# Second layer's output projection: seven block products for the heads' rows, on scaled float16 pairs

## The chip, the cores and the metric

The kernel runs on one core of one Trainium2 chip. Its engines work side by side, each through its own queue in order: TensorE (PE) multiplies, VectorE (DVE), ScalarE (ACT) and GpSimd (POOL) work elementwise, SyncE (SP) issues most of the DMAs. The metric is the device time of one execution in microseconds (us); three timed runs of the kernel before gave a median of 1188.93 us (1188.14 to 1191.31). The profile is of one further execution.

## The reference

Two layers of a decoder with 1024 tokens and width 1024. Layer 1 has as its main part a forgetting attention of 16 heads, and beside it a cross-attention of 4 heads into 256 memory tokens. Both are gated, joined and projected:

```python
def mixer_sublayer(x, mem, w_in, w_mem_kv, w_out, main_fn):
    h = x @ w_in
    ...
    y_main = main_fn(u_main)                       # (1024, 1024)
    y_mem = memory_attention(q_mem, mem, w_mem_kv) # (1024, 512)
    y = jnp.concatenate([y_main * jax.nn.silu(g_main), y_mem * jax.nn.silu(g_mem)], axis=-1)
    return y @ w_out                               # w_out: (1536, 1024)

# each layer
x = layer_norm(ALPHA * x + y, ln_g[layer], ln_b[layer])
```

All is float32. `w_out` has 1024 rows for the heads and 512 rows for the memory's heads.

## The kernel before

A float32 product is made of three products of lower precision: each operand is split into a high part and a rest, and high x high, high x rest and rest x high are summed in one PSUM bank. Two splits are in use. `hi_lo` (L195) makes a float32r high part (ACT), a bfloat16 rest (DVE, L199) and a bfloat16 copy of the whole (ACT or POOL). `scaled_hi_lo` (L170) multiplies by a power of two and makes two float16 tensors: ACT writes the high part (L171), DVE the rest (L172). The projections of layer 1 and the attention use float16 pairs; both output projections use `hi_lo`.

`OutProj` (L560) is the output projection. The contraction over 1536 rows of `w_out` is 12 tiles of 128 rows, in three groups `c`: 0 and 1 are the heads, 2 is the memory. The tokens are eight tiles of 128, taken as four pairs `sp`; the columns are two halves of 512 (`nh`). For one pair, four PSUM banks (two tiles x two halves) each collect 12 x 3 matmuls of 128x128 by 128x512: 144 per pair, 576 in all (L615). The gated results `y` go through DRAM (`y1d`) and come back transposed to the projection as tiles of `T`; `w_out` comes in pieces of 128x512 (`fetch_two`, L569) and is split one piece at a time (`split`, L584). When a pair is done, `norm` (L691) adds ALPHA times the residual, takes the statistics (bn_stats on DVE), and applies scale and shift in two DVE instructions of 128x1024 (L710, L712), then a DMA writes the rows out.

In layer 1 the projection begins inside the attention: `fox` (L1174) runs 16 heads and a last stretch of six steps, in which the first pair's memory products (`early`) are laid between the attention's last products. PE's order is written out by hand there (`manual_schedule`); instructions under `keep_in_program_order` are pinned on their engine; the rest is ordered by the framework's scheduler. After `fox`, `rest` (L643) runs the other products in the order pair 0: c 0, then pair 1: c 2, pair 0: c 1, pair 1: c 0 and 1, then pairs 2 and 3. PSUM banks come from named pools: `pj` (2 banks), `L` (3), `T` (2), `O` (1).

The last head pair's result `o` (a tile of `G`) is made by ACT (L1148) and DVE (L1149) out of bank `O`, gated on POOL (L1158, in `pair_out`), and stored to `y1d`.

Of the kernel before, what the change touches and what calls it, by code (L numbers as in the profile page):

```python
# [9 lines left out]
F32 = mybir.dt.float32  # L10
# [8 lines left out]
P = 128  # L19
# [16 lines left out]
LAG = 6  # L36
# [42 lines left out]
def trunk_kernel(ctx, tc, x, xT, memT, win, wk, wv0, wv, wmk, wmv, wout, poolw, pscale, lng, lnb, bforget, out):  # L79
# [30 lines left out]
    def G(shape=(P, S), dt=F32):  # L110
        return sb(list(shape), "G", 4, dt)
# [157 lines left out]
    def power_of(to, m, least):  # L269

        nc.vector.tensor_scalar(m, m, least, None, ALU.max)
        nc.vector.tensor_scalar(to.bitcast(I32), m.bitcast(I32), 0x7F800000, None, ALU.bitwise_and)

    scales = const.tile([P, 20], F32, name="scales")
    ex, sx, sq, unq, unv0, unv, tmp, tmp2 = (scales[:, k : k + 1] for k in range(8))
    ews, sws, un1s, hun1s = ([scales[:, 8 + 3 * k + g : 9 + 3 * k + g] for g in range(3)] for k in range(4))
# [24 lines left out]
    def scales_of_weights(g):  # L301

        m = highest[:, g : g + 1]
        ew, sw, un1, hun1 = ews[g], sws[g], un1s[g], hun1s[g]
        power_of(ew, m, 2.0 ** -24)
        nc.vector.reciprocal(sw, ew)
        nc.vector.tensor_scalar(sw, sw, 2.0 ** 12, None, ALU.mult)
        nc.vector.tensor_tensor(un1, ex, ew, ALU.mult)
        if g == 1:
            nc.vector.tensor_tensor(unq, un1, un1, ALU.mult)  # L310
            nc.vector.tensor_scalar(unq, unq, 2.0 ** -19, None, ALU.mult)
            nc.vector.reciprocal(sq, unq)
        nc.vector.tensor_scalar(un1, un1, 2.0 ** -25, None, ALU.mult)
        nc.vector.tensor_scalar(hun1, un1, 0.5, None, ALU.mult)
        if g == 2:
            for un, a in ((unv0, un1s[1]), (unv, un1)):
                nc.vector.tensor_tensor(un, a, un1, ALU.mult)
                nc.vector.tensor_scalar(un, un, 2.0, None, ALU.mult)

# [240 lines left out]
    class OutProj:  # L560
# [82 lines left out]
        def rest(self, resid, X, dst):  # L643
# [14 lines left out]
            for sp, c in order:  # L658
# [21 lines left out]
                if X is not None and c == 0 and sp in (1, 2):  # L680
                    keep(sp - 1)
                if c == 1:
                    norm(sp, accs.pop(sp), gb, zs, X, dst)

    def rows_of(resid, sp):
        zs = [G() for _ in range(2)]
        for a, z in enumerate(zs):
            tc.keep_in_program_order(nc.sync.dma_start(z, resid[(2 * sp + a) * P : (2 * sp + a + 1) * P, :]))
        return zs

    def norm(sp, accs, gb, zs, X, dst):  # L691
        for a in range(2):
            s = 2 * sp + a
            rows = slice(s * P, (s + 1) * P)
            z = zs[a]
            stats = tiny(12)
            for nh in range(2):
                zn = z[:, nh * NH : (nh + 1) * NH]
                nc.vector.scalar_tensor_tensor(zn, zn, ALPHA, accs[a][nh], ALU.mult, ALU.add)  # L699
                nc.vector.bn_stats(stats[:, 6 * nh : 6 * nh + 6], zn)  # L700
# [7 lines left out]
            nc.vector.tensor_tensor(r, r, t, ALU.mult)  # L708
            for cols in (slice(0, NH), slice(NH, D)) if s == ST - 1 else (slice(0, D),):
# [126 lines left out]
    with tc.tile_pool(name="in1", bufs=1) as in1:  # L836
# [317 lines left out]
        def pair_out(pr, c, o, g):  # L1154

            for k in (2 * c + 1, 2 * c) if g is not None else ():
# [17 lines left out]
        def fox(following, out_proj, head):  # L1174
# [8 lines left out]
            for hd in range(HEADS + 1):  # L1183
# [16 lines left out]
                for i in range(ST if hd < HEADS else LAG):  # L1200
# [40 lines left out]
                    else:  # L1241
                        inverse()
                        behind()
                        out_proj.split(11 + i, True, gp_copy)
                        if i > 1:
                            out_proj.fetch_two(two_lines(4 + 2 * i))
                    if pr == 7:
                        out_proj.split((0, 0, 0, 0, 1, 3, 4, 6, 6, 6, 6, 6, 7, 8, 9, 10)[step], True, gp_copy)
# [5 lines left out]
                    if hd == HEADS and i == LAG - 1:  # L1254
                        out_proj.begin()
# [10 lines left out]
        wtags = [("B", 10), ("V", 4), ("MK", 4)] + [("B", 10)] * 3 + [("w", 0), ("MK", 4), ("R", 2), ("V", 4), ("PG", 0), ("B", 10)]  # L1266
        out_proj = OutProj(1, w_slots(wtags, in1), y1d)
# [10 lines left out]
        out_proj.rest(x1, None, out)  # L1278
# [61 lines left out]
```

## Time and profile before

| | |
|---|---|
| median of three timed runs | 1188.93 us |
| profiled execution, first to last instruction | 1185.0 us |
| what lies around the span in a timed run (1188.93 - 1185.0) | 3.9 us |
| PE, ACT, DVE, POOL busy | 1162.7, 685.3, 780.6, 288.0 us |
| layer 0's output projection on PE | about 340 to 462 us |
| the attention's last product | about 1057 us |
| the last output product | about 1175 us |

The device time of the profiled execution itself is not listed apart from its span. A busy PE need not be a PE at its peak, so spacing of matmuls is read from the starts of consecutive rows. The chain of work that ended last follows PE through the whole of the last 120 us: 48 of its 75 longest pieces after 1044 us are runs of L615, and only the last layer norm stands behind it.

### The profile page before, as it was taken

The numbers are of one execution on the slowest core, as the hardware profiler recorded it, in microseconds if no ns is written. First come the engines' busy times: TensorE is split into PE (matmuls) and PEld (weight loads), VectorE is DVE, ScalarE is ACT, GpSimd is POOL, SyncE is SP. The second block draws the span as 40 slices with busy tenths as digits, with TensorE's granted clock in tenths as the row PEclk, the third lists the DMA queues.
The fourth block names the chain that finished last, engine by engine and source line by source line (L and its number), as shares of the span: only waits on it lengthen the run. The fifth ranks groups of instructions, "written<-read, shape, count | busy, mean of one in ns | idle before, by whom it ended". The sixth has DMA issues, their size and how long they took to land. (4 is left out here: it accounts for less than half of the span.)

```text
span 1185.0 us, 19799 instructions
## 1 busy us (share of the span) xinstructions
PE 1162.7 (98%) x6894; PEld 671.8 (57%) x6941; DVE 780.6 (66%) x1841; ACT 685.3 (58%) x1514; POOL 288.0 (24%) x441
## 2 busy tenths in 40 slices
PE   8999999999999999999999999999999999999996
PEld 5566766555555557556674555555555545455553
DVE  5744675555765557457655888778877788874654
ACT  6578875876563234467422776667766767674210
POOL 4322001310000000000011554555545444750000
PEclk9999999999999999999999999999999999999999
DMA  7576647754285554445824889979996899975430
GB/s 264 183 243 195 166 103 211 249 178 152 90 274 167 153 156 125 120 142 109 214 109 122 180 196 201 199 169 194 208 203 146 168 197 203 218 182 176 173 112 36
DMA packets 286196, 203.89 MB, mean 172 GB/s; under 512 B 224912, under 2 KB 238352, under 8 KB 286096
## 3 DMA queue, kind: packets, MB, share of 16 engines
q1 hardware_dynamic: 279120, 179.49, 60.5%
q0 software_dynamic: 6976, 23.14, 6.0%
q8 instruction: 54, 0.88, 0.3%
q14 instruction: 46, 0.38, 0.1%
HBM read 116.01 MB, written 22.61 MB: 117 GB/s over the span
## 5 line engine op out<-in xcount | busy, mean ns | idle before, releaser
L359 PE MATMUL pj<-A,w 128*128 128x512 f16 (+2 forms) x2827 | 650.9, 383 | 1.7 <-DVE Y L376 0.2
L359 PEld LDWEIGHTS <-w 128*128 128x128 f16 (+1 forms) x2560 | 245.6, 98 | 277.0 <-issue 8.0
L1076 ACT ACTIVATE T<-MK,s 128x512 f32<-128x512 f32 x192 | 111.2, 579 | 66.6 <-DVE s L1068 49.6
L1105 DVE SCALAR_TENSOR_TENSOR P<-T,s,P 128x512 f16<-128x512 f32 x192 | 112.1, 613 | 39.1 <-ACT P L1104 38.2
L1104 ACT ACTIVATE P<-T,s 128x512 f16<-128x512 f32 x192 | 103.2, 576 | 53.3 <-issue 28.9
L615 PEld LDWEIGHTS <-T 128*128 128x128 bf16 x736 | 70.7, 98 | 87.5 <-issue 4.4
L1042 POOL TENSOR_SCALAR_AFFINE_SELECT raw<-R 128x256 f32<-128x256 f32 (+3 forms) x128 | 60.1, 471 | 180.3 <-DVE s L1068 99.3
L323 PE MATMUL L<-A 128*128 128x512 f16 (+3 forms) x384 | 84.7, 326 | 5.7 <-DVE s L1068 5.6
L199 DVE TENSOR_TENSOR w<-raw,w 128x512 bf16<-128x512 f32 x74 | 51.9, 701 | 58.0 <-ACT w L198 39.3
L556 POOL DMA_DIRECT2D y1d<-V x4 | 2.1, 536 | 336.5 <-DVE V L534 330.6
L359 PEld LDWEIGHTS pj<-A,w 128*128 128x128 f32 x352 | 65.1, 188 | 17.0 <-ACT w L198 1.5
L199 DVE TENSOR_TENSOR T<-T,T 128x1024 bf16<-128x1024 f32 x22 | 26.8, 1220 | 67.0 <-PE pj L615 36.3
L323 PEld LDWEIGHTS <-A 128*128 128x128 f16 x384 | 37.4, 98 | 49.1 <-issue 7.8
L178 POOL TENSOR_TENSOR w<-B,w 128x512 f16<-128x512 f32 x54 | 62.9, 1166 | 4.0
L198 ACT CAST w<-raw 128x512 fp32r<-128x512 f32 x76 | 46.7, 615 | 23.9 <-DMA raw<-in_win_dram 8.7
L1130 PEld LDWEIGHTS <-V 128*64 128x64 f16 (+1 forms) x1152 | 50.6, 104 | 13.0 <-issue 5.6
L1130 PE MATMUL O<-T,V 128*64 128x128 f16 (+1 forms) x1152 | 57.5, 220 | 0.1
L198 ACT CAST T<-T 128x1024 fp32r<-128x1024 f32 x22 | 23.1, 1048 | 59.7 <-DMA T<-y1d 30.6
L615 PE MATMUL pj<-B,T 128*128 128x512 bf16 (+1 forms) x187 | 52.1, 385 | 0.3
L1068 DVE CUSTOM_DVE_ANT_0 MK<-L,R,scales 128x512 f32<-128x512 f32 x64 | 45.3, 708 | 9.4 <-PE L L323 9.1
L200 ACT CAST w<-raw 128x512 bf16<-128x512 f32 x78 | 48.2, 618 | 3.3 <-PE pj L359 1.9
L615 PE MATMUL L<-B,T 128*128 128x512 bf16 (+1 forms) x165 | 47.0, 394 | 0.2
(296 smaller groups left out, 1856.3 us busy)
## 6 DMA issues: line engine op xcount, KB each, us to landing
raw<-in_win_dram SPq DMA_DIRECT2D x66, 256.0 KB, 3.4
W<-in_win_dram POOLq DMA_DIRECT2D x48, 256.0 KB, 4.2
R<-cumd SPq DMA_DIRECT2D x16, 512.0 KB, 4.6
B<-in_win_dram SPq DMA_DIRECT2D x15, 512.0 KB, 5.5
y0d<-Y SPq DMA_DIRECT2D x12, 512.0 KB, 4.3
raw<-in_wout_dram SPq DMA_DIRECT2D x24, 256.0 KB, 2.8
T<-y0d SPq DMA_DIRECT2D x12, 512.0 KB, 4.6
A<-A SPq DMA_DIRECT2D x24, 256.0 KB, 4.0
```

Source lines behind the costliest of these rows:

```text
L178: pin(nc.gpsimd.tensor_tensor(to.lo, src, to.hi, ALU.subtract))
L198: pin(nc.scalar.copy(to.hi, src))
L199: pin(nc.vector.tensor_tensor(to.lo, src, to.hi.bitcast(F32), ALU.subtract))
L200: pin((top or nc.scalar.copy)(to.top, src))
L323: nc.tensor.matmul(acc, a, b, start=i == 0, stop=i == len(terms) - 1)
L359: nc.tensor.matmul(accs[n], a[:, k, :], b[:, pc * 4 + k, n * NH : (n + 1) * NH], start=seen[n] == 1, stop=seen[n] == 3 * KT,)
L615: nc.tensor.matmul(accs[a][nh], y, w, start=kt == 8 and i == 0, stop=kt == 7 and i == 2,)
L1042: tc.keep_in_program_order(nc.gpsimd.affine_select(C[:, :w], R[:, lo:up], [[-1, w]], ALU.is_ge, -NEG, base=w - P, channel_multiplier=1,))
L1076: nc.scalar.activation(e, p[:, lo:up], AF.Exp, bias=top, scale=-1.0, accum_out=sums[:, n, hd % 2, i : i + 1],)
L1104: nc.scalar.activation(pair[:, lo:up], e, AF.Copy, scale=r)
L1105: nc.vector.scalar_tensor_tensor(pair[:, L + lo : L + up], e, r, pair[:, lo:up], ALU.mult, ALU.subtract)
L1130: nc.tensor.matmul(acc[rows, (i % 4) * P : (i % 4) * P + P], v[:, b, 2 * j : 2 * j + (1 if e else 2), :].rearrange("p e d -> p (e d)"), pt ...
```

## The change

Layer 1's heads' part of the output projection, 1024 rows of `w_out` against all tokens, is computed by Strassen's scheme (Winograd's form). For a token pair, `y` is a 2x2 of blocks (two token tiles x two halves of 512 contracted rows), `w_out` a 2x2 of blocks (two halves of the rows x two halves of the columns). Seven products of blocks replace eight, each of 12 matmuls (4 tiles of 128 rows x 3 parts): 84 per pair instead of 96, with float16 pairs as operands. The memory's 512 rows are computed as before (48 matmuls per pair).

Class `Seven` replaces `OutProj` in layer 1. What is added:

- `pass_of_w_out`, `scale_of_w_out`: in layer 0's output projection, the heads' 16 pieces of `w_out[1]` are loaded once more, summed in absolute value on ACT, and made into one scale for all (`over_partitions`: a transpose and a small product on PE).
- `four`, `block`, `split_last`: from each four pieces of `w_out`, the sums t1 to t4 in place (POOL, for one of four groups DVE), then each of the 28 blocks into a float16 pair (ACT and DVE).
- `rows`: for a token pair, load `y`, sum its absolute values on ACT, a scale for the pair through PE, four sums s1 to s4 on POOL, and seven float16 pairs (ACT and DVE).
- `seven`: the products and their sums into the rows `z` on DVE.
- `normed(..., spread=True)`: ACT applies mean and scale, POOL gain and bias (two instructions of 128x1024), for all tiles but the last.
- The last pair's own last rows come straight from `o`, and the memory products of pairs 1 to 3 run before the seven.

```diff
+    def pass_of_w_out(k):
+        r = lines[0][:, k % 4, :].bitcast(F32)
+        nc.sync.dma_start(r, wout[1, k % 2, k // 2])
+        nc.scalar.activation(r, r, AF.Abs, accum_out=sums_out[:, k : k + 1])
+    def over_partitions(to, m, bank, r, pin=lambda ins: ins):
+        t = ps([P, 4, P], *bank)
+        nc.tensor.transpose(t[:1, 0, :], m, ident)
+        pin(nc.vector.tensor_reduce(r[:1], t[:1, 0, :], AX.X, ALU.max))
+        yield
+        nc.tensor.matmul(t[:, 1, :1], ones[:1], r[:1], start=True, stop=True)
+        pin(nc.vector.tensor_copy(to, t[:, 1, :1]))
...
+        def four(self):
+            b11, b12, b21, b22 = (self.raws.pop(0) for _ in range(4))
+            self.fours = {"11": b11, "t3": b12, "21": b21, "22": b22, "t2": b11, "t4": b21, "t1": b22}
+            self.gp(b12, b22, b12)
+            return self.fours
...
+        def block(self, b, f, by=None):
...
+            pin(nc.scalar.activation(to.hi, r, AF.Copy, scale=swo))
+            pin(nc.vector.scalar_tensor_tensor(to.lo, r, swo, to.hi, ALU.mult, ALU.subtract))
+            self.w7[b].append(to)
+            if b == "11":
+                self.gp(f["t2"], f["t3"], f["11"], ALU.add, by)
...
+        def split_last(self):
+            fs = [self.four() for _ in range(2)]
+            for b in self.BLOCKS:
+                for f, by in zip(fs, (nc.gpsimd, nc.vector)):
+                    self.block(b, f, by)
+                yield
...
+        def rows(self, sp):
+            if sp == 0:
+                y = self.first
+                nc.sync.dma_start(y[1][:, 3, :], self.last[:, : 2 * P])
+            else:
+                y = [self.load(c, sp) for c in range(2)]
...
+            for c, part in enumerate((y[0], y[1][:, :3, :], y[1][:, 3, :])):
...
+                pin(nc.scalar.activation(seen, part, AF.Abs, accum_out=m[:, c : c + 1]))
...
+            yield from over_partitions(mx, mx, ("L", 3), r, pin)
...
+            gp(s1, a21, a22, ALU.add)
+            gp(s2, s1, a11)
+            gp(s4, a12, s2)
+            gp(s3, a11, a21)
...
+                scaled_hi_lo(halves[b], t, sy, pin)
+        def product(self, y, w):
+            self.turn += 1
+            acc = ps([P, NH], *(("L", 3) if self.turn % 3 == 0 else ("pj", 2)))
...
+        def seven(self, sp, z, between):
...
+            add = lambda to, p, t: nc.vector.scalar_tensor_tensor(to, p, un, t, ALU.mult, ALU.add)
+            p = self.product(y["11"], w["11"])
+            nc.scalar.activation(u, p, AF.Copy, scale=un)
+            add(z11, p, z11)
+            between(0)
+            add(z11, self.product(y["12"], w["21"]), z11)
...
+            add(u, self.product(y["s2"], w["t2"]), u)
+            nc.vector.tensor_tensor(z12, z12, u, ALU.add)
...
+            add(v, self.product(y["s3"], w["t3"]), u)
+            nc.vector.tensor_tensor(z22, z22, v, ALU.add)
+            nc.vector.tensor_tensor(z21, z21, v, ALU.add)
...
+        def rest(self, resid, dst):
...
+            def opened(sp, accs):
+                zs = rows_of(resid, sp, make[sp])
+                for a in range(2):
+                    for nh in range(2):
+                        zn = zs[a][:, nh * NH : (nh + 1) * NH]
+                        nc.vector.scalar_tensor_tensor(zn, zn, ALPHA, accs[a][nh], ALU.mult, ALU.add)
+                return zs
...
+                for sp in range(n):
+                    self.seven(sp, zs[sp], lambda k, sp=sp: between(sp, k))
+                    normed_two(sp)
...
+            if spread:
...
+                        nc.scalar.activation(z[:, cols], z[:, cols], AF.Identity, bias=t, scale=r)
+                        nc.gpsimd.tensor_tensor(z[:, cols], z[:, cols], gb[0][:, cols], ALU.mult)
+                        nc.gpsimd.tensor_tensor(z[:, cols], z[:, cols], gb[1][:, cols], ALU.add)
```

How the rows of two engines stand now. **DVE, around the second pair.** Before, DVE's rows while PE multiplies for a pair are those of the previous pair's norm: additions out of a bank (L699), statistics (L700 to L708) and the two long applications (L710, L712).

```order
L702 BN_AGGR s_12838<-s_12833 128x2
L703 TENSOR_SCALAR s_12839<-s_12838 128x1
L710 SCALAR_TENSOR_TENSOR G_12781<-G_12781,s_12838,P_12722 128x1024
L699 SCALAR_TENSOR_TENSOR G_12782<-G_12782,L_12456 128x512
L705 RECIPROCAL s_12841<-s_12840 128x1
L699 SCALAR_TENSOR_TENSOR G_12782<-G_12782,pj_12457 128x512
L706 TENSOR_SCALAR s_12842<-s_12841,s_12839 128x1
L700 BN_STATS s_12853<-G_12782 128x6
```

Now, in the second pair's products (banks `L_` and `pj_`), the additions out of a bank (L905), the rests of the third pair's operands (L172, into the big tile `A_12641`) and the sums (L915 to L923) stand in one row:

```order
L172 SCALAR_TENSOR_TENSOR A_12641<-raw_13139,yscales,A_12641 128x512
L905 SCALAR_TENSOR_TENSOR P_13186<-pj_13246,yscales,P_13186 128x512
L915 TENSOR_TENSOR A_3343<-A_3343,P_13186 128x512
L172 SCALAR_TENSOR_TENSOR A_12641<-raw_13138,yscales,A_12641 128x512
L905 SCALAR_TENSOR_TENSOR A_3343<-L_13263,yscales,A_3343 128x512 x2
L335 TENSOR_REDUCE yscales<-L_13278 1x1
L172 SCALAR_TENSOR_TENSOR A_12641<-raw_13140,yscales,A_12641 128x512
L1026 BN_STATS s_13330<-A_3343 128x6
L905 SCALAR_TENSOR_TENSOR P_13186<-pj_13283,yscales,P_13186 128x512
L1028 BN_AGGR s_13333<-s_13330 128x2
L922 TENSOR_TENSOR A_3343<-A_3343,P_13186 128x512
L923 TENSOR_TENSOR A_3343<-A_3343,P_13186 128x512
```

The long applications (the second, L712, stands a few rows on) are gone from DVE; additions and rests have come, and a bank is given back only in this row's order.

**POOL, from the attention's end on.** Before, these are its last rows: gatings (L1171, L1158) and bfloat16 copies of `w_out` (L193); it then has nothing to the end.

```order
L1171 TENSOR_TENSOR R_12191<-R_12191,G_12052 128x256 x4
L193 TENSOR_SCALAR B_12450<-A_3341 128x512 x2
L1158 TENSOR_TENSOR G_11585<-G_11585,G_11344 128x256 x2
L193 TENSOR_SCALAR w_12532<-A_3341 128x512
L193 TENSOR_SCALAR w_12534<-A_3341 128x512
L193 TENSOR_SCALAR MK_12567<-A_3341 128x512 x2
```

Now its last rows are the sums of `y` (L874; of the third and fourth pair here) and gain and bias of the norm (L1044, L1045; token tiles 0 and 1 here, six more behind):

```order
L874 TENSOR_TENSOR raw_13138<-T_13018,T_13020 128x512
L874 TENSOR_TENSOR raw_13139<-raw_13138,T_13018 128x512
L874 TENSOR_TENSOR raw_13141<-T_13020,raw_13139 128x512
L874 TENSOR_TENSOR raw_13140<-T_13018 128x512
L1044 TENSOR_TENSOR G_12686<-G_12686,P_12998 128x1024
L1045 TENSOR_TENSOR G_12686<-G_12686,P_13000 128x1024
L874 TENSOR_TENSOR raw_13322<-T_13202,T_13204 128x512
L1044 TENSOR_TENSOR G_12687<-G_12687,P_12998 128x1024
L1045 TENSOR_TENSOR G_12687<-G_12687,P_13000 128x1024
L874 TENSOR_TENSOR raw_13323<-raw_13322,T_13202 128x512
```

POOL works to the end of the program now, on operands that all lie in SBUF.

**DVE, while PE multiplies the memory's rows of pairs 2 and 3.** Before, DVE had here only rests of operands and the first norm (L199, then L699):

```order
L199 TENSOR_TENSOR G_12707<-A_3341,P_12706 128x512 x2
L199 TENSOR_TENSOR B_12715<-A_3341,B_12714 128x512 x2
L199 TENSOR_TENSOR T_12776<-T_12774,T_12775 128x1024
L199 TENSOR_TENSOR T_12875<-T_12873,T_12874 128x1024
L199 TENSOR_TENSOR T_12930<-T_12928,T_12929 128x1024
L699 SCALAR_TENSOR_TENSOR G_12781<-G_12781,L_12454 128x512
```

Now the row waits at L335 for PE's transpose, and behind it stand rests of `w_out`'s blocks (L778), a weight sum (L769), an addition of the memory's part (L944) and the scale of the pair (L338 to L871); the first pair's own operands (L172) come a few rows on:

```order
L335 TENSOR_REDUCE yscales<-L_12813 1x1
L778 SCALAR_TENSOR_TENSOR R_12816<-A_3343,scales,R_12816 128x512 x2
L769 TENSOR_TENSOR A_3343<-A_3343 128x512
L944 SCALAR_TENSOR_TENSOR G_12866<-G_12866,pj_12762 128x512
L338 COPY yscales<-L_12813 128x1
L271 TENSOR_SCALAR yscales<-yscales 128x1
L272 TENSOR_SCALAR yscales<-yscales 128x1
L869 RECIPROCAL yscales<-yscales 128x1
L870 TENSOR_SCALAR yscales<-yscales 128x1
L871 TENSOR_SCALAR yscales<-yscales,scales 128x1
L778 SCALAR_TENSOR_TENSOR R_12848<-A_3343,scales,R_12848 128x512 x2
```

What stood beside the end of the matmuls is now work that the first product waits for.

More of the change, by code (lines that the diff above doesn't have):

```diff
@@ L687, in rows_of @@
+    def rows_of(resid, sp, make=G):
+        zs = [make() for _ in range(2)]
         for a, z in enumerate(zs):
@@ L692, in norm @@
         for a in range(2):
-            s = 2 * sp + a
-            rows = slice(s * P, (s + 1) * P)
             z = zs[a]
-            stats = tiny(12)
             for nh in range(2):
@@ L1154, in pair_out @@
         def pair_out(pr, c, o, g):
-            for k in (2 * c + 1, 2 * c) if g is not None else ():
+            if pr == 7 and c == 0:
+                out_proj.own(o)
+            for k in ((0, 1) if pr == 7 and c == 0 else (2 * c + 1, 2 * c)) if g is not None else ():
                 cols = slice(k * 2 * P, (k + 1) * 2 * P)
@@ L1277, in trunk_kernel @@
             low[0] = False
-        out_proj.rest(x1, None, out)
+        out_proj.rest(x1, out)
 _INS = [
```

256 lines of the change are left out of this document (241 added, 15 removed).

## The prediction

> **What bounds the kernel now.** I read the page first, then busy time by stretches, then the chain of work that ended last, and single rows of the last 130 us. The page and two stretches (columns after start, end and length: busy us and count of PE, weight loads, DVE, ACT, POOL; granted clock; DMA share; GB/s):
>
> ```profile
> span 1185.0 us, 19799 instructions
> PE 1162.7 (98%) x6894; PEld 671.8 (57%) x6941; DVE 780.6 (66%) x1841; ACT 685.3 (58%) x1514; POOL 288.0 (24%) x441
> ...
> 400.00:500.00 100.00, 99.72 (x521) 59.36 (x525) 58.63 (x108) 41.95 (x70) 0.00 (x0) 1.00 0.54 148
> 1076.00:1185.00 109.00, 99.47 (x444) 56.44 (x450) 57.73 (x107) 21.02 (x27) 0.00 (x0) 0.98 0.31 111
> ```
>
> PE is busy to the last 9 us; in the last 109 us DVE works 58, ACT 21, POOL nothing. So the span here is a count of matmuls plus a last norm. What one matmul costs is the distance of starts, in the chain and in the row behind the attention's last product:
>
> ```profile
> 1056.88 1.12 PE L1130 MATMUL O<-T,V 128*128 128x128 f16 x20
> 1057.93 0.60 PE L615 MATMUL pj<-V,B 128*128 128x512 bf16 x2
> ...
> 1061.74 0.93 PE pj L615 x4
> 1062.67 1.74 PE L L615 x8
> 1064.42 1.73 PE pj L615 x8
> ...
> 1175.31 0.59 PE L615 MATMUL pj<-B,T 128*128 128x512 bf16 x2
> ```
>
> Four high parts (float32r) take 0.93, so 0.2325 each; eight others 1.73, so 0.216. Of the 576 matmuls, 44 of the first 48 lie before 1057.9. The rest (176 high, 352 others, four left over 0.9) comes to 1057.9 + 0.9 + 40.9 + 76.0 = 1175.7, and the last row ends at 1175.9: the projection runs without a gap. Behind it stand 9.3 us: the last norm and the way out.
>
> ```profile
> 1176.78 0.67 DVE L699 SCALAR_TENSOR_TENSOR G<-G,pj 128x512 f32<-128x512 f32 x1
> 1180.60 1.41 DVE L712 SCALAR_TENSOR_TENSOR G<-G,s,P 128x512 f32<-128x512 f32 x2
> ```
>
> DVE ends at 1182.0, the span at 1185.0: 3.0 for the last store.
>
> **PE's part of the change.** Per pair go 96 heads' matmuls (32 x 0.2325 + 64 x 0.216 = 21.3); 84 float16 ones come at 0.216 (18.1). Four pairs: -12.5 us. Two small products per pair for its scale cost about the weight load below, 0.2 each: +1.6.
>
> ```profile
> L359 PEld LDWEIGHTS pj<-A,w 128*128 128x128 f32 x352 | 65.1, 188 | 17.0 <-ACT w L198 1.5 <-DVE Y L376 0.7
> ```
>
> In time: 1058.8, then memory's rows of three pairs (3 x 10.6), small products 0.8: the first block product could begin at 1091.5; 28 x 12 x 0.216 = 72.6 and 0.8 more end at 1164.9. The tail in the new row is about 9.5 (one application more between the last addition and the last store, 0.7; the second half of the tile before it is already under way). **If PE goes on setting the end: 1174.4**, 10.6 us less.
>
> **What covers the preparation.** The last head's values leave their bank as before:
>
> ```profile
> 1061.61 0.68 ACT L1148 ACTIVATE G<-O,scales 64x512 f32<-64x512 f32 x1
> 1062.32 0.76 DVE L1149 SCALAR_TENSOR_TENSOR G<-O,scales,G 64x512 f32<-64x512 f32 x1 [0.43 <-ACT G L1148]
> 1063.16 2.37 POOL L1158 TENSOR_TENSOR G<-G,G 128x256 f32<-128x256 f32 x2 [5.53 <-DVE G L1149]
> A<-A SPq DMA_DIRECT2D x24, 256.0 KB, 4.0
> ```
>
> The own rows can land at about 1065.5 + 4.0 = 1069.5 on SP's queue (behind them there only loads of x and later y), their absolute sum and its reduction take another 1; PE asks for the transpose at 1058.8 + 10.6 + 6.3 (28 of the third pair's matmuls) = 1075.7. Five us are left, so this chain costs nothing; without PE's memory products in front it would cost some 12. Rests and high parts of `w_out`'s blocks were there as `hi_lo` before. ACT has room for all of it (21 of 109 us before).
>
> **DVE's part.** From 1076 its row is fixed, and a bank is free for PE only when its addition is done; `pj` gives PE two products (5.2 us) of grace. Prices, by starts of consecutive rows:
>
> ```profile
> 473.39 1.40 DVE L172 SCALAR_TENSOR_TENSOR w<-raw,scales,w 128x512 f16<-128x512 f32 x2
> 449.16 1.29 DVE L199 TENSOR_TENSOR T<-raw,T 128x512 bf16<-128x512 f32 x2 [2.65 <-PE pj L615]
> L1089 DVE RECIPROCAL s<-s 128x1 f32<-128x1 f32 x128 | 20.7, 162 | 2.8
> ```
>
> Two scaled operations take 1.40, the second 0.66; two plain ones 1.29, the second 0.60; a small one 0.16. Ahead of the first addition of a product: 12 rests of weights and 7 of `y` (19 x 0.66 = 12.5), 8 plain (4.8), 15 small (2.4): 19.7, to 1095.7. A round of seven products: 8 additions and 7 rests (9.9), 3 sums and 4 statistics (4.3), 23 small (3.7): 17.9, against PE's 18.5. Two rounds, a third without a scale (16.4), and the fourth's first addition (0.7): 1148.6. Left to itself DVE keeps up.
>
> But POOL now works beside it, which it did not here before. What this does shows at four places:
>
> ```profile
> 706.94 1.41 POOL L1158 TENSOR_TENSOR G<-G,G 128x256 f32<-128x256 f32 x2 [2.79 <-DVE G L1149]
> ...
> 1064.00 0.94 DVE L199 TENSOR_TENSOR R<-A,R 128x512 bf16<-128x512 f32 x1 [0.20 <-ACT R L198]
> 1065.04 1.04 DVE L199 TENSOR_TENSOR V<-A,V 128x512 bf16<-128x512 f32 x1
> ...
> 1014.92 3.27 DVE L199 TENSOR_TENSOR MK<-A,MK 128x512 bf16<-128x512 f32 x2
> ...
> 1014.93 2.72 POOL L178 TENSOR_TENSOR w<-B,w 128x512 f16<-128x512 f32 x2
> L178 POOL TENSOR_TENSOR w<-B,w 128x512 f16<-128x512 f32 x54 | 62.9, 1166 | 4.0
> ```
>
> POOL's two gatings took 1.41 alone and 2.37 beside DVE (the row at 1063.16, quoted above). DVE's operation issued at 1065.04 took 1.04 and not 0.69: POOL was busy until 1065.53, and from there it is 0.55. At 1014.9 two of each, 1.29 and about 2.3 alone, end 3.27 later: nearly the sum. Additions from PSUM (L699, L376) show no such thing. So a DVE operation with both inputs in SBUF and a POOL operation take turns. The Trainium skill, "SBUF — State Buffer", section "Who interferes with whom", says that a Vector instruction with two SBUF inputs contends with a GpSimd instruction that reads SBUF, and that the later one waits until the first is finished; the trace agrees (1.04 against 0.69), and by a rule of shared bandwidth instead DVE would lose little here and the time would be that of the first rival.
>
> After the change DVE has 51 such operations from 1076 to that addition (12 + 28 rests, 11 sums), and POOL 22 instructions: 14 of 128x512 (two weight sums, twelve sums of `y`) and 8 of 128x1024 (norm of four tiles). The trace has no float32 one of either size. 128x512 lies between 1.17 (L178, a float16 input) and 2 x 0.705 = 1.41; I take 1.2. 128x1024 lies between 2.1 (on along the line from 0.705 to 1.17) and 2.8 (4 x 0.705); I take 2.3, by the nearer 128x512 row. "GPSIMD Engine Reference", section 3.1, of the Trainium skill has 4.497 us for 2048 columns; halved and quartered it would make the sum 1.5 us less in POOL's time, an estimate. Each POOL instruction can stop DVE once. At nothing PE's 1174.4 stands; at its full length 14 x 1.2 + 8 x 2.3 = 35.2; at half its length, a DVE operation coming at any moment of it, 17.6. Going through the two rows side by side from the rests at 1076 I find 21, since POOL's sums are released by the rest before, and the next rest stands right behind them. I take **20**: the fourth pair's first addition at 1168.6. Its last four products (10.4) follow, and the tail: 1168.6 + 10.4 + 9.5 = **1188.5**.
>
> **Layer 0.** 16 absolute sums on ACT come into its output projection. One is about the exponential with its accumulator:
>
> ```profile
> L1076 ACT ACTIVATE T<-MK,s 128x512 f32<-128x512 f32 x80 | 55.0, 687 | 43.6 <-DVE s L1068 35.2 <-DVE P L1105 8.3
> L1076 ACT ACTIVATION_READ_ACCUMULATOR T<-MK,s 128x1 f32 x192 | 36.5, 190 | 0.1
> 379.74 1.04 ACT L198 CAST T<-T 128x1024 fp32r<-128x1024 f32 x1 [3.64 <-DMA T<-y0d]
> ```
>
> That is 14 us of ACT, which is idle 58 of 100 us there (400 to 500). A cast stands behind each; the casts wait 3.64 for their load anyway, whose issue on SP now stands behind loads of `w_out`. Between 0 and 14 I take 1, by that row's slack.
>
> **Sum.** 1188.5 + 1.0 = 1189.5 against 1185.0; with the 3.9 us that a timed run has beyond the span (1188.93 - 1185.0), **1193.4**. A measurement here tells about 0.3% from no change, that is 1185.4 to 1192.5.
>
> **The rivals.**
> *PE stays the bound* (not slower). POOL's instructions mostly fall where DVE waits for PE or ACT anyway, or hold it for less. It decides below 11 us of DVE's waiting: the time is 1179 (1174.4 + 1.0 + 3.9) up to 1184.5. For it: DVE's own sum leaves PE 6 us of room. Against it: the row is so dense (17.9 of 18.5 in a round) that a wait has little idle time to fall into.
> *Half of it*: 11 to 17 us of waiting, 1184.5 to 1190.4.
> *Layer 0's passes stall PE*: loads of `y0d` come late behind those of `w_out`, each of the 16 passes costs its 0.88; from two thirds of it (9) on it hides any gain, 1190 to 1207. Against it: the slack above.
> POOL as the last engine I give no chance of its own: its last two halves (1.2 each) follow the seventh tile's statistics, well ahead of the eighth's store.
>
> **How the numbers follow.** DVE held up by POOL, 17 to 30 us, centre 20: 0.46. PE the bound: 0.25. Half of it: 0.21. Layer 0: 0.08. Slower by over 0.3% takes most of the first and last: 0.44; within: the third and the first's lower edge, 0.28; faster: 0.28. The range reaches down to PE's bound, 1179, and up to 30 us of waiting with layer 0's 1, 1204.
>
> **What would show it.** Right: in the last 95 us DVE near 95% busy, its rests (L172, L778) well over 0.75 us on the mean, PE waiting for DVE at `pj` in the second and third pair, POOL's 128x512 sums above 1.2. Wrong: rests at 0.75, PE without gaps from 1058 to 1165, the seven products' spacing 0.216; or PE waiting for ACT before 460.

## The result, and the profile after

The changed kernel is slower: a median of 1207.46 us (1205.48 to 1209.88, five runs) against 1188.14 (1184.81 to 1191.31, five runs) for the kernel before on the same chip, a ratio of 1.0161 [1.0141, 1.0181]. The prediction said 1193.4, in a range up to 1204. The direction was right, the size was not: 4.5 us were expected, 19 came.

Page and stretches of the profile after; the columns of the stretches are those of the first fence of the prediction:

```profile
span 1203.8 us, 20044 instructions
PE 1163.3 (97%) x6908; PEld 658.8 (55%) x6908; DVE 847.0 (70%) x1954; ACT 720.2 (60%) x1597; POOL 360.1 (30%) x476
...
400.00:500.00 100.00, 99.19 (x510) 58.95 (x508) 60.12 (x116) 38.90 (x63) 0.00 (x0) 1.00 0.54 140
1058.00:1110.00 52.00, 46.62 (x213) 24.28 (x211) 50.57 (x69) 30.70 (x53) 35.64 (x24) 0.93 0.68 219
1110.00:1200.00 90.00, 73.11 (x329) 32.28 (x326) 83.75 (x162) 30.32 (x53) 44.16 (x22) 0.94 0.11 42
```

The shares of the whole span hardly moved. The last stretches did: DVE is busy 134.3 of 142 us, PE waits, and POOL, idle in the last 109 us of before, works 80. In the same execution PE's rows give the times of the stages, here the attention's last product, the first block product and the last ones:

```profile
1062.81 1.12 PE L1469 MATMUL O<-T,V 128*128 128x128 f16 x20
...
1106.82 0.38 PE L895 MATMUL pj<-B,A 128*128 128x512 f16 x1
...
1190.29 0.59 PE L895 MATMUL pj<-B,A 128*128 128x512 f16 x2
```

| us | predicted | after | e2 | e3 | e9 | e15 |
|---|---|---|---|---|---|---|
| start of layer 0's output projection | 331.8 | 334.6 | 332.4 | 334.0 | 332.6 | 332.3 |
| from there to the attention's last product | 726.1 | 728.2 | 728.7 | 728.1 | 731.2 | 727.5 |
| from there to the last block product's end | 122.1 | 128.1 | 119.7 | 114.8 | 111.8 | 110.8 |
| from there to the end | 9.5 | 12.9 | 9.9 | 9.9 | 9.9 | 9.9 |
| span | 1189.5 | 1203.8 | 1190.7 | 1186.7 | 1185.5 | 1180.5 |

(e2 to e15 are experiments below.) The first line lies ahead of every edit and scatters by 3 us between executions, so 2.8 of the 14.3 us of span that were missed are chance. The rest: 2.1 between layer 0's projection and the attention's end (a stretch that reads 727.5 in e15 too, where layer 0 has no passes, so what layer 0 costs is taken from medians below), 6.0 in the preparation and the block products, 3.4 in the tail. What lies between span and median, 3.9 in the prediction, is 3.7 here; that the two agree is luck. The result lists a time and a span for each run of the changed kernel, and these lie 1.7 us apart (1205.48 and 1203.8 for the execution shown); the rest of the 3.7 is that this execution was faster than the median.

What PE waited for from 1058 on (engine and line that waited, what for, us in total, times, longest):

```profile
PE L L337 <- DVE yscales L335: 7.1, 3, 2.5
PE pj L895 <- DVE G L905: 2.5, 2, 2.3
PE pj L895 <- DVE A L905: 1.3, 1, 1.3
PE L L334 <- DVE yscales L864: 1.2, 1, 1.2
```

The greatest is one that the prediction had at nothing: the small product of a pair's scale, behind DVE's reduction L335. DVE's two-input operations from 1110 to 1204, by form (busy us, mean ns of one):

```profile
L172 DVE SCALAR_TENSOR_TENSOR A<-raw,yscales,A 128x512 f16<-128x512 f32 x12 | 13.0, 1080 | 0.5 <-ACT A L171 0.5
L172 DVE SCALAR_TENSOR_TENSOR A<-T,yscales,A 128x512 f16<-128x512 f32 x9 | 6.5, 743 | 0.0
L1034 DVE TENSOR_TENSOR s<-s,s 128x1 f32<-128x1 f32 x8 | 6.2, 776 | 0.1
L915 DVE TENSOR_TENSOR A<-A,P 128x512 f32<-128x512 f32 x2 | 4.4, 2208 | 0.1
L1036 DVE SCALAR_TENSOR_TENSOR s<-s,s 128x1 f32<-128x1 f32 x7 | 4.2, 601 | 0.1
```

The rests that read `raw` take 1.08 instead of 0.74, and multiplying two columns of one number each takes 0.78. One moment shows why, DVE first, then POOL:

```profile
1132.61 1.78 DVE L172 SCALAR_TENSOR_TENSOR A<-raw,yscales,A 128x512 f16<-128x512 f32 x1
1134.49 2.13 DVE L1034 TENSOR_TENSOR s<-s,s 128x1 f32<-128x1 f32 x1
1136.65 1.19 DVE L1036 SCALAR_TENSOR_TENSOR s<-s,s 128x1 f32<-128x1 f32 x1
...
1131.47 2.37 POOL L1044 TENSOR_TENSOR G<-G,P 128x1024 f32<-128x1024 f32 x1 [7.89 <-ACT G L1043]
1133.92 2.68 POOL L1045 TENSOR_TENSOR G<-G,P 128x1024 f32<-128x1024 f32 x1
1136.56 1.26 POOL L874 TENSOR_TENSOR raw<-T,T 128x512 f32<-128x512 f32 x1
```

The rest at 1132.61 ends (1134.39) 0.55 behind POOL's multiplication (1133.84), the column at 1134.49 ends (1136.62) with POOL's addition (1136.60), the next (1137.84) with POOL's sum (1137.82). Each waits until the POOL instruction that was there before it has ended.

Where "held" is said below, it is the time of DVE's operations with two inputs in SBUF beyond their time in the run with the least POOL work (0.744 for a rest, 0.69 for a plain operation on 128x512, 0.148 for the columns of L1034 and L1036). After: 30.5 us from 1040 to the end, 24.6 of them from 1076, 17.7 from 1110.

### The profile page after: what moved, and what is told of

Read it like the earlier page. It is cut to its first block, busy times and chain, and to the rows that moved or that the text cites. A ratio compares the mean times of both kernels' runs of the same rounds, so it can differ in the third digit from the quotient of the medians.

```text
span 1203.8 us, 20044 instructions
## 1 busy us (share of the span) xinstructions
PE 1163.3 (97%) x6908; PEld 658.8 (55%) x6908; DVE 847.0 (70%) x1954; ACT 720.2 (60%) x1597; POOL 360.1 (30%) x476
## 5 line engine op out<-in xcount | busy, mean ns | idle before, releaser
L199 DVE TENSOR_TENSOR w<-raw,w 128x512 bf16<-128x512 f32 x74 | 52.3, 707 | 60.7 <-ACT w L198 39.6
L352 PEld LDWEIGHTS <-A 128*128 128x128 f16 x384 | 37.4, 98 | 49.3 <-issue 8.1
L644 PEld LDWEIGHTS <-T 128*128 128x128 bf16 x384 | 36.9, 98 | 45.8 <-issue 1.9
L895 PEld LDWEIGHTS <-A 128*128 128x128 f16 x336 | 33.1, 99 | 44.8 <-issue 7.5
L1469 PEld LDWEIGHTS <-V 128*64 128x64 f16 (+1 forms) x1152 | 50.6, 104 | 12.9 <-issue 6.0
L258 POOL DMA_DIRECT2D W<-in_win_dram x48 | 26.5, 553 | 55.9 <-ACT W L267 44.2
L540 ACT ACTIVATE P<-L,s 128x256 f32<-128x256 f32 x64 | 29.5, 472 | 22.9 <-DVE s L537 19.4
L267 ACT ACTIVATE W<-W 128x512 f32<-128x512 f32 (+1 forms) x68 | 42.2, 623 | 0.0
```

Of the source, the lines that this page charges most:

```text
L199: pin(nc.vector.tensor_tensor(to.lo, src, to.hi.bitcast(F32), ALU.subtract))
L352: nc.tensor.matmul(acc, a, b, start=i == 0, stop=i == len(terms) - 1)
L1469: nc.tensor.matmul(acc[rows, (i % 4) * P : (i % 4) * P + P], v[:, b, 2 * j : 2 * j + (1 if e else 2), :].rearrange("p e d -> p (e d)"), pt ...
```

## The experiments

The theory: DVE is the last engine, and POOL's instructions hold it. Rivals: layer 0's passes; PE's half clock behind its pauses; DVE's own load, whatever POOL does. All are the changed kernel with the edit shown; ratios are to the kernel before, run beside them on the same chip.

**e1_scalar** gives the two columns' operations a form with one tensor input and a scalar pointer.

```diff
-            nc.vector.tensor_tensor(r, r, t, ALU.mult)
+            nc.vector.tensor_scalar(r, r, t, None, ALU.mult) if X is None else nc.vector.tensor_tensor(r, r, t, ALU.mult)
...
-                nc.vector.scalar_tensor_tensor(t, mv[:, 0:1], -1.0, r, ALU.mult, ALU.mult)
+                nc.vector.tensor_scalar(t, mv[:, 0:1], r, -1.0, ALU.mult, ALU.mult)
```

> The two 128x1 operations of the norm with two SBUF tensors as inputs (L1034, L1036) take one of them as a scalar operand instead; same values. Theory A (a DVE operation with two SBUF tensor inputs waits for POOL's running instruction): in the changed kernel these 15 rows took 0.78 and 0.60 us on the mean where a small operation takes 0.15, 8.2 us in all; here they fall to 0.15-0.2 each, some of the wait is inherited by the next rest, the time is 1199.5 to 1203.5. Rival B (the DVE row is late by its own length and by PE's handshake, POOL only fills waits): no change, 1205.5 to 1209.

1205.61 us, 1.0151 [1.0136, 1.0166]: some 2 us less, within the runs' spread. DVE's groups of e1 after 1058:

```profile
L172 DVE SCALAR_TENSOR_TENSOR A<-raw,yscales,A 128x512 f16<-128x512 f32 x16 | 18.8, 1175 | 0.0
L172 DVE SCALAR_TENSOR_TENSOR A<-T,yscales,A 128x512 f16<-128x512 f32 x9 | 10.9, 1227 | 0.0
...
L1034 DVE TENSOR_SCALAR s<-s,s 128x1 f32<-128x1 f32 x8 | 1.6, 204 | 0.2
```

The columns are free (0.204), but the rests that read `T` went from 0.743 to 1.227. From 1110 on the held time is some 17, after 17.7. The wait belongs to POOL's instruction; the next two-input operation inherits it. The theory had expected less inheritance: its range for the time is missed, and the time alone lies in the rival's. What speaks against that rival is e2.

**e2_no_gain**: POOL's gain and bias left out.

```diff
-                        nc.gpsimd.tensor_tensor(z[:, cols], z[:, cols], gb[0][:, cols], ALU.mult)
-                        nc.gpsimd.tensor_tensor(z[:, cols], z[:, cols], gb[1][:, cols], ALU.add)
+                        pass
+                        pass
```

> Leaves out gain and bias of the last norm for the first six token tiles and the first half of the seventh (POOL's 14 instructions L1044, L1045). Theory A: DVE operations were lengthened by 24.7 us from 1076 us on, of which about 14 beside these instructions; DVE's row gets shorter by 10 to 14: 1193 to 1198. Rival B: POOL is off the chain that sets the end; 1205 to 1209.

**e3_pool_silent**: as e2, and `y`'s sums s1 to s4 left out as well.

```diff
-            s1, s2, s3, s4 = (raw([P, 4, P]) for _ in range(4))
...
-            gp(s1, a21, a22, ALU.add)
-            gp(s2, s1, a11)
-            gp(s4, a12, s2)
-            gp(s3, a11, a21)
+            s1, s2, s3, s4 = a21, a11, a11, a12
...
```

> Leaves out, beside that, the sums s1 to s4 of y on POOL (its operands go into the products as they are). Theory A: another 4 to 6 us less than e2_no_gain, DVE's rests at 0.66 to 0.75: 1187 to 1193; no lower than PE's own count allows, about 1182. Rival B: 1205 to 1209.

e2: 1192.41, 1.0039 [1.0026, 1.0052]. e3: 1188.37, 1.001 [0.9997, 1.0023]. Both lie below the rival's 1205. Gain and bias are worth 15.1 us, the sums of `y` 4.0. In e3 the rests (DVE's group after 1058) and the stretch from 1110 to 1180, where DVE holds nobody, read:

```profile
L172 DVE SCALAR_TENSOR_TENSOR A<-T,yscales,A 128x512 f16<-128x512 f32 x21 | 15.4, 744 | 0.5 <-ACT A L171 0.5
...
1110.00:1180.00 70.00, 66.78 (x311) 30.20 (x309) 59.68 (x147) 26.26 (x47) 0.00 (x0) 1.00 0.11 46
```

The block products take 73.7 without a wait of PE among them; the prediction's count was 73.4. Left to itself DVE does keep up.

**e4_no_passes**: layer 0's loads and sums of `w_out[1]` left out, a constant in their place.

```diff
-        nc.sync.dma_start(r, wout[1, k % 2, k // 2])
-        nc.scalar.activation(r, r, AF.Abs, accum_out=sums_out[:, k : k + 1])
+        pass
+        pass
```

> Leaves out the 16 passes over w_out in layer 0 (a constant takes the place of their sums, so the scale is the same). By the trace of the changed kernel (PE waits 1.79 at 371.5 for an addition behind a square root that stands behind four passes, and starts layer 1's projection 3.7 us later relative to the start of layer 0's projection): 3 to 4 us less, 1203.5 to 1204.5. By the prediction's term of 1 us: 1206.5. Rival: the later part absorbs it (DVE's row there is released by loads, not by PE): no change, 1207.5.

1203.41, 1.0139 [1.0121, 1.0156]: 4.0 us less, not 1, though the runs of either kernel spread over 4 to 5 us. In the rows of after (ACT, DVE, PE) stands what the passes do:

```profile
368.46 0.63 ACT L327 ACTIVATE A<-A 128x512 f32<-128x512 f32 x1 [0.42 <-DMA A<-in_wout_dram]
369.20 1.28 ACT L1030 ACT_TABLE_LOAD   x1
370.50 0.20 ACT L1030 ACTIVATE s<-s 128x1 f32<-128x1 f32 x1
...
370.73 0.17 DVE L1031 RECIPROCAL s<-s 128x1 f32<-128x1 f32 x1 [2.33 <-ACT s L1030]
...
371.54 1.19 PE L644 MATMUL pj<-B,T 128*128 128x512 f32 x4 [1.79 <-DVE G L1019]
```

A norm's square root stands behind a pass and, with it, behind a table load of 1.28; DVE's reciprocal waits 2.33, its next additions are late, and PE waits 1.79 for the bank. In before that table load stood at 360.68, where ACT was idle, 3.4 us ahead of its square root. The casts, where the prediction looked, are not in it. The 1.79 is less than half of the 4.0; where the rest lies the trace doesn't show.

**e5_warm**: a dozen products without use ahead of three of the four pairs' L337, so that PE does not pause.

```diff
...
+            for _ in range(12):
+                nc.tensor.matmul(spot, f[:, :P], f, start=True, stop=True)
         nc.tensor.matmul(t[:, 1, :1], ones[:1], r[:1], start=True, stop=True)
```

> Twelve matmuls (2.6 us) into an unused bank stand in PE's row ahead of three of the four small products that wait for L335, so that PE works through these waits. In the changed kernel the granted clock was 0.50 from 1088 to 1092 us and low again from 1148 to 1152, each time behind a pause of 2.6 to 3 us; matmuls there are spaced 0.43 instead of 0.216, about 6 us in two places. Here: clock 1.0 in both stretches. If PE's lost clock sets the end: 1201 to 1203. If DVE's row sets it (theory A): 1206 to 1208.

1208.78, 1.0178 [1.016, 1.0195]: nothing won, and the theory's range ended at 1208. Stretches of after, then of e5 (granted clock in the third column from the right):

```profile
1088.00:1092.00 4.00, 4.00 (x10) 1.55 (x10) 3.83 (x9) 0.00 (x0) 1.62 (x1) 0.50 1.01 378
...
1087.00:1092.00 5.00, 4.93 (x23) 2.68 (x24) 4.83 (x12) 0.89 (x2) 1.66 (x2) 1.00 1.03 384
1106.60:1110.00 3.40, 3.40 (x10) 1.22 (x8) 3.30 (x12) 0.00 (x0) 1.96 (x1) 0.50 0.49 154
...
1164.00:1172.00 8.00, 3.77 (x11) 1.35 (x11) 7.97 (x9) 1.82 (x3) 2.88 (x2) 0.57 0.18 69
```

The clock stays at 1.00 where it was low in after, and is low elsewhere: behind a pause of 2.2 between large products (1103.65 to 1105.81), and around one of 8.18 that ends at 1168.23, where PE waits for DVE's addition L908. The mean granted clock of the execution is 0.989 in both. So the edit moves the half clock and doesn't remove it, and this run can't tell what half clock costs. The rows of after tell more: behind the first low stretch PE waits 2.31 for DVE (at 1106.07), behind the second 2.29 (at 1162.91), and from 1058 on DVE waits for PE only twice, 1.08 at 1117.38 and 0.45 at 1119.97. DVE's row sets the pace there, and faster products would have waited longer.

**e7_dve_norm** takes gain and bias back to two DVE instructions for every tile, as in before. **e8_dve_passes** makes layer 0's sums on DVE. **e10_norm_passes** does both.

```diff
-                    normed(2 * sp + a, zs[sp][a], gb, None, dst, 2 * sp + a < ST - 1)
+                    normed(2 * sp + a, zs[sp][a], gb, None, dst)
...
-        nc.scalar.activation(r, r, AF.Abs, accum_out=sums_out[:, k : k + 1])
+        nc.vector.tensor_reduce(sums_out[:, k : k + 1], r, AX.X, ALU.add, apply_absolute_value=True)
```

> The norm of all tiles in two DVE instructions as in the kernel before (L1049, L1051); none of it on ACT and POOL. Adds some 13 x 1.2 = 16 us to DVE's row and takes POOL's 14 long instructions away. Theory A: e2_no_gain's 1192.4 plus what of the 16 us does not fit into the 13 us in which DVE stood idle there from 1110 us on: 1194 to 1200. Rival (work on DVE costs as much as POOL's holds): 1205 to 1209.

> Layer 0's 16 absolute sums on DVE instead of ACT; nothing left out. If they cost time because a square root stands behind them on ACT (and a table load with it), the time is that of e4_no_passes, 1203 to 1205. If the loads of w_out in front of y0d are what costs: 1207.

> e7_dve_norm and e8_dve_passes together: norm in two DVE instructions, layer 0's absolute sums on DVE. The two gains (12.5 and 2.5 us) lie in different stages and add up: 1191.5 to 1193.5. If the later stage absorbs the earlier one's gain: 1195.

e7: 1195.0, 1.006 [1.0044, 1.0076]: 12.5 us less, though DVE gets two more instructions per tile. e8: 1204.97, 1.0145 [1.0125, 1.0166], 2.5 less, inside the spread of its runs (1202.65 to 1207.46); the wait of 1.79 is gone, and one of 1.33 for the loads of `y0d` came. e10: 1199.34, 1.0082 [1.005, 1.0113], slower than e7 alone, but its four runs lie 8 us apart (1192.7 to 1201.07) and the profiled one is the fastest. Why they scatter is open.

**e9_pool_out**: as e3, and the blocks' sums t1 to t4 left out. **e15_floor**: as e9, without the passes, and PE asking later for the pairs' scales. Together they look for what is left when POOL does next to nothing.

```diff
-            self.gp(b12, b22, b12)
...
-                self.gp(f["t2"], f["t3"], f["11"], ALU.add, by)
...
```

> e3_pool_silent with the sums t1 to t4 of w_out's blocks left out too, on POOL and DVE: POOL does nothing but the last gates from 1045 us on. In e3_pool_silent PE lost 6.7 us between the attention's end and the first block product (waits for L335 at 1086.6 and 1102.3, a low clock between) and none in the block products. If that loss comes from rests held up by POOL's weight sums (1.4 us for two of 0.66): 1181 to 1184. If it comes from the order of DVE's row: 1187 to 1189.

> e9_pool_out without layer 0's passes (a constant in their place) and with PE asking later for the two scales: gain and bias of six and a half tiles, the sums of y and of w_out's blocks and the passes are left out, what stays is PE's part of the change. The prediction put this bound at 1179. If the pieces taken out one by one add up: e9's 1185.3 less 4 for the passes, less 0 to 3 for PE's waits, 1178.5 to 1181.5. If something else in the new order costs PE time: 1184 or more.

e9: 1185.31, 0.9974 [0.9965, 0.9984], between its two ranges. e15: 1181.77, 0.9944 [0.993, 0.9958]. The floor that the prediction put at 1179 exists, 2.5 us higher. But it is without POOL's work, the passes and the early question.

**e11_later**: as e10, and PE asks later for the scales of the first two pairs: ten matmuls later for the first, and behind the first block product for the second.

```diff
-                run(islice(units, 10))
+                run(islice(units, 20))
                 next(rows[0])
...
-                        if k == 0:
-                            next(rows[sp + 1])
+                        for _ in range((2 if sp == 0 else 1) if k == 0 else 0):
+                            next(rows[sp + 1])
```

> As e10_norm_passes, and PE asks later for the scales of the first two pairs: ten memory matmuls more ahead of the first small product that waits for L335, and the second one behind the first block product. In e7_dve_norm PE waited there 2.2 and 2.35 us and ran 4 us at half clock. If DVE's row (50.7 of 52 us busy there) sets the first block product: within 1.5 us of e10_norm_passes. If PE's waits and clock do: 4 to 7 us less.

**e12_sums_dve**: as e11, with all of POOL's sums on DVE.

```diff
-            tc.keep_in_program_order((by or nc.gpsimd).tensor_tensor(to, u, v, op))
+            tc.keep_in_program_order(nc.vector.tensor_tensor(to, u, v, op))
```

> As e11_later, with POOL's sums of w_out's blocks and of y (12 and 16 of 128x512) on DVE. Adds 28 x 0.6 = 17 us to DVE's row; DVE operations were lengthened by 14.4 + 0.9 us in e7_dve_norm from 1040 us on, and that goes. Theory A (a POOL instruction beside DVE costs DVE about half its length, 0.6 of 1.2 to 1.7, what the same sum costs DVE itself): within 3 us of e11_later, rests at 0.66 to 0.75. Rival (POOL's sums are mostly hidden): 8 us or more above it.

e11: 1194.58, 1.0053 [1.0038, 1.0068], the same as e7 within the spread; PE's wait moved to L334, 3.9 us for L864. By its own rule the 4.8 below e10's median would speak for PE's waits; but e10's runs scatter over 8 us, and the one with the profile took 1192.7, so e11 doesn't decide between its two theories. e12: 1201.24, 1.0111 [1.009, 1.0132], 6.7 more than e11, between what the two theories gave. The stretches of e11, then e12:

```profile
1110.00:1180.00 70.00, 66.80 (x310) 29.97 (x309) 69.76 (x146) 21.96 (x43) 10.54 (x8) 1.00 0.12 46
...
1110.00:1180.00 70.00, 63.61 (x285) 28.06 (x283) 69.86 (x151) 21.95 (x43) 0.00 (x0) 0.95 0.10 38
```

In both DVE has no idle time left: in e11 by its own work with almost no POOL beside it, in e12 by that work and the sums. Once gain and bias are back, DVE's load is the bound, and POOL's sums cost less than DVE would need for them.

**e13_pieces**: gain and bias on POOL as in the change, in pieces of 128x256.

```diff
+                        for q in range(cols.start, cols.stop, 2 * P):
+                            for v, op in zip(gb, (ALU.mult, ALU.add)):
+                                nc.gpsimd.tensor_tensor(z[:, q : q + 2 * P], z[:, q : q + 2 * P], v[:, q : q + 2 * P], op)
```

> The changed kernel with gain and bias on POOL in four pieces of 128x256 instead of one of 128x1024 (0.7 instead of 2.3 to 2.7 us each, in sum longer). If a DVE operation waits only for the POOL instruction that runs, the wait falls with its length: 17.7 us of lengthening from 1110 us on become 8 to 11, the time 1198 to 1202. If POOL's total time counts, or POOL goes first while it has work: 1207 to 1211.

1203.76, 1.0129 [1.0112, 1.0145], 3.7 less, between its two ranges. The held time behind 1110 falls from 17.7 to 11.1, so short pieces hold less; yet DVE is idle for 9.8 us there instead of 5.2. Of this 2.4 lie at 1111.51, where DVE and ACT wait for a first block product that PE ran at half clock. Why no more was won is not shown.

**e14_act_stats**: as e11, the mean and the mean square of six tiles by ACT's accumulators instead of DVE's bn_stats.

```diff
+                nc.scalar.activation(seen, z, AF.Copy, scale=1.0 / D, accum_out=mv[:, 0:1])
+                nc.scalar.activation(seen, z, AF.Square, scale=D ** -0.5, accum_out=mv[:, 1:2])
...
```

> As e11_later, and the norm's sums of six token tiles (mean and mean square) as two ACT passes of 128x1024 with an accumulator instead of two statistics of 128x512 and their aggregate on DVE. In e11_later DVE had no idle time from 1110 us on. If its row is what still keeps that kernel above the kernel before: about 6 x 1.1 = 6.6 us less, 1187.5 to 1190. If ACT's queue (rests wait for high parts behind these passes) takes its place: 1193 to 1197.

**e16_best**: as e14, the second pair's question still later, and the passes' loads on POOL's queue.

```diff
-                    if k == 4:
+                    if k == 6:
                         next(rows[1])
...
-        nc.sync.dma_start(r, wout[1, k % 2, k // 2])
+        nc.gpsimd.dma_start(r, wout[1, k % 2, k // 2])
```

> e14_act_stats with two orders changed: the transpose for the second pair's scale stands behind the last memory matmuls on PE (it waited 4.17 us for L864 there, ahead of 14 matmuls and the first block product), and layer 0's loads of w_out go through POOL's queue instead of SP's (PE waited 2.16 us for a cast behind a late load of y0d). If PE's place in the order holds the first block product back: it starts 3 to 4 us earlier and the time is 1186 to 1189. If DVE's row does (50.7 of 52 us busy from 1058 to 1110): 1190.5 to 1192.5.

e14: 1192.26, 1.0034 [1.0022, 1.0046], 2.3 less than e11 where 6.6 were expected. e16: 1201.47, 1.0109 [1.009, 1.0129], worse than e14. Both of its edits show in their own stage: in layer 0 PE now waits four times, 1.14 to 1.84 us, and the wait for L335 grew (PE's row of e16):

```profile
1115.87 0.58 PE L337 MATMUL L<-yscales,ones 1*128 1x1 f32 x2 [7.59 <-DVE yscales L335]
```

The later question puts L335 behind three pairs of rests (L778) that take 2.4 us each, and more rests between them (1106.55 to 1115.54). The first block product did start earlier, 38.2 us behind the attention's last product instead of 42.7 in e14; the wait takes more than that back. No kernel that does the whole work was faster than the one before.

## Why the prediction missed the size

Taking parts away one after the other gives an account in medians: e15 1181.8; the passes and the early question +3.5 (e9); sums of blocks on POOL +3.1 (e3); sums of `y` +4.0 (e2); gain and bias +15.1 (after, 1207.5). The shares hold in this order of removal, and each ratio's interval is some 1.2 to 2.4 us either way.

**Right.** The mechanism and its place: POOL, newly beside DVE, holds its operations with two inputs in SBUF, and DVE's row sets the end. The Trainium skill, "SBUF — State Buffer", section "Who interferes with whom", calls the shared port pair an exclusive lock; e1's wait that passes on and the column of 2.13 us agree. PE's count came (73.4 against 73.7 in e3), and so did the price of POOL's sums (1.2 taken; 1.27 alone in after). Ahead of the fourth pair's first addition 20 us of holding were taken and 20.4 measured.

Of the signs, DVE near 95% (93% from 1110), longer rests, POOL's longer sums and waits at `pj` came. The mean of L172 from 1110 is 0.94, but not in both its forms: rests that read `T` stayed at 0.743, since POOL's instructions fell on the rests of `raw` and on the columns. That additions out of a bank are not held ("L699, L376") rested in before on L376 alone, since POOL did nothing during any L699; in after it holds, 0.74 for L905 as in e3.

**The steps that failed.**

"Five us are left, so this chain costs nothing." It put the pair's own rows and their sum against PE's products, and left out DVE's row ahead of L335. The rows of after around the question, DVE, then POOL, then PE:

```profile
1077.19 2.97 DVE L778 SCALAR_TENSOR_TENSOR MK<-A,scales,MK 128x512 f16<-128x512 f32 x2 [0.42 <-ACT MK L777]
1080.26 1.58 DVE L769 TENSOR_TENSOR A<-A 128x512 f32<-128x512 f32 x1
...
1087.15 0.27 DVE L335 TENSOR_REDUCE yscales<-L 1x1 f32<-1x128 f32 x1
...
1076.18 3.43 POOL L769 TENSOR_TENSOR A<-A 128x512 f32<-128x512 f32 x2
1079.58 1.72 POOL L874 TENSOR_TENSOR raw<-A 128x512 f32<-128x512 f32 x1
...
1087.48 0.58 PE L337 MATMUL L<-yscales,ones 1*128 1x1 f32 x2 [2.22 <-DVE yscales L335]
```

Two rests took 2.97 instead of 1.40 and the plain sum 1.58 instead of some 0.7, beside POOL's sums of blocks: 2.4 us of holding in two rows. DVE reached L335 at 1087.15, and PE stood for 2.22. But the holding is not what makes this wait: in e9 the sums of blocks are left out, the same two rests take 1.41, and PE waits 1.95 at the same place (e9's rows, DVE, then PE; L943 there is L944 of after):

```profile
1082.26 1.28 DVE L943 SCALAR_TENSOR_TENSOR A<-A,T 128x512 f32<-128x512 f32 x2 [2.90 <-DMA A<-x]
...
1084.63 1.22 DVE L199 TENSOR_TENSOR T<-T,T 128x1024 bf16<-128x1024 f32 x1
...
1087.56 0.27 DVE L335 TENSOR_REDUCE yscales<-L 1x1 f32<-1x128 f32 x1
...
1087.89 0.38 PE L337 MATMUL L<-yscales,ones 1*128 1x1 f32 x2 [1.95 <-DVE yscales L335]
```

Six additions of the memory's part and a rest on 128x1024 stand ahead of L335, in after from 1081.94 to 1087.15, and the first of them needs a load of `x`: in e9 DVE comes there early and waits 2.90 for it. So the order of DVE's row makes this wait, with POOL or without. PE waits again for the second and the fourth pair's scale, 2.31 and 2.53, and these depend on POOL's work: the second is 3.80 in e2, 0.88 in e3 and gone in e9, the fourth is gone in e2. How much time the three waits cost stays open, since DVE had work throughout them and e11, which asks later, decides nothing.

"DVE has 51 such operations from 1076 to that addition." The count started at 1076 and ended at the fourth pair's first addition. Of 30.5 us held, 5.9 lie before it and 4.2 behind it, where the prediction had none. It left out the columns L1034 and L1036, which are small but have two SBUF inputs and were held for 8.3 us, 6.7 of them inside the count's stretch: that the sum of 20 was met without them is in part luck. By e1 freeing them changes who waits and hardly how long.

"At half its length": as a sum over POOL's instructions up to there that was right, 20.4 for 20, but those behind the fourth pair's first addition were given nothing. The tail took 12.9 instead of 9.5 (9.9 in e2): the last norms stand behind DVE's late row. In e7, with gain and bias on DVE, it still takes 12.1, with DVE idle for only 1.5 us from 1110 on: DVE's lateness is enough for it.

"Between 0 and 14 I take 1": the passes cost some 4 by medians (e4). What PE's row shows of it, 1.79, came through the square root's queue on ACT; the slack was read at the casts.

**The rivals.** PE as the bound falls; its floor, e15, needs POOL's work, the passes and the early question gone. Layer 0's passes were too dear at 9 and cost some 4. Each missed term alone is small; they added up because they come one behind the other, in layer 0, before the first block product, in DVE's row and in the tail.

What stays open: why e10's runs scatter, where the passes' other 2 us lie, what PE's half clock costs in runs where DVE waits for PE, and how the 6.0 us before and in the block products divide between the late scale and the holds, which share DVE's row.

## What to carry to other kernels

Before work goes to an idle POOL, count on DVE's row every operation with two SBUF inputs, however small, over the whole stretch in which POOL works, and where DVE has no slack, count a part of POOL's time as lost. That part differed here, in the order in which the pieces were taken out: gain and bias are 34.0 us of POOL (360.1 against 326.1 in e2) and cost 15.1, the sums of `y` are 24.6 (301.5 in e3) and cost 4.0. Moving one operation out of the way mostly hands its wait to the next. A change that takes 10.6 us from the bound engine by adding work to two others needs their rows worked out from the first operation that the bound engine asks for: a cheap reduction costs what stands ahead of it in its queue.

## What the runs showed of the hardware

Short pauses of PE can halve its granted clock. In after, between large products, the small L337 apart, PE pauses for 2.7 us (to 1087.99), 2.6 (to 1106.38), 2.8 (to 1148.40) and 2.3 (to 1162.91). Behind the first and the third the clock is 0.50 and 0.57 over the next 4 us, behind the second and the fourth it is 1.00 (the first stretch stands under e5; the columns as in the first fence):

```profile
1148.30:1152.30 4.00, 4.00 (x13) 1.55 (x13) 4.00 (x8) 0.00 (x0) 1.27 (x1) 0.57 0.00 0
...
1106.40:1110.00 3.60, 3.60 (x18) 1.66 (x18) 3.60 (x10) 0.39 (x1) 2.39 (x1) 1.00 0.42 134
1163.00:1167.00 4.00, 4.00 (x19) 1.76 (x19) 3.97 (x6) 2.26 (x4) 3.92 (x2) 1.00 0.17 67
```

The Trainium skill, "TensorE: Matmul & The Clock Gate", section "What's actually happening", has an idle window of about 3.4 us that runs freely. Here shorter pauses, of 2.7 and 2.8 and in e5 of 2.2 us, were enough, and the measurement decides. Since 2.6 and 2.3 left the clock at 1.00, the length of a pause alone doesn't decide it.

A DVE operation on 128x1, 0.15 alone, can take 2.13 behind POOL, as long as one on 128x512 (L915, 2.06 at 1142.79): the wait depends on POOL's instruction and not on DVE's.
